# A tuned transformer-trunk kernel on one core: sums asked for later, V turned earlier, last rows normalised from halves

## The chip, the core and the metric

The kernel runs on one core of one Trainium2 chip. The metric is the device time of one launch in microseconds (us). The core's engines are TensorE (PE, with PEld for its weight loads), VectorE (DVE), ScalarE (ACT), GpSimd (POOL) and SyncE (SP, which here only starts transfers). ACT and POOL can start transfers too. A queue with a `q` behind the engine's name (SPq, POOLq) is the instruction stream that starts transfers.

## The reference

One layer over x of 2048 rows and 1024 columns, in fp32; `S` is 2048 and `D` 1024.

```python
mod = silu(c) @ w_ada + b_ada;  shift, scale, gate = split(mod, 3)
u = x * (1 + scale) + shift
q, k, v, a_gate, p_in, p_gate, m_a, m_p = split(u @ w_in)     # widths 1024 128 128 1024 1024 1024 1024 1024
a = sliding_window_sink_attention(q, k, v) * silu(a_gate)     # 16 heads of 64, 2 kv heads, window 128
p = (group_linear(multiscale_causal_pool(p_in), w_pool_mix) * pool_scale) * silu(p_gate)
y = sigmoid(m_a) * (a @ w_attn_proj) + sigmoid(m_p) * (p @ w_pool_proj)
y = (y @ w_out) * (1 + gate)
out = layer_norm(2**0.25 * x + y) * ln_gain + ln_bias
```

## The kernel before

**Products.** Every fp32 matrix is split into a high and a low part (fp32r), and a product of two 128x128x512 blocks is three matmuls (`mm3`: high by high, high by low, low by high). A large product is done in 2x2 blocks with seven products instead of eight. The class `Quad` (L262) holds the weights of one such 2x2 piece: two row tiles of 128 by 1024 columns, loaded by `load` (L270) as two pieces into a tile `W` (three blocks of 128x512) and one, the lower right one, into `A22` (the trace calls it `A`). `sum1` (L280, on POOL) adds two blocks, `mid` (L284, L285) subtracts twice and loads the fourth block by POOL's queue (L286), `late` (L290) subtracts once more. `pair_split` casts two blocks to the high part on ACT (L312) and takes the low part on DVE (L128) into `w_set`; `half_split` does so for `A22` (L319). `product` then runs twelve matmuls against one of seven resident moving sets (B11, T1, T2, B21, T3, B22, T4) in SBUF: `set_B` and `set_T` in the trace. There are two `W` and two `A22` buffers. `A22` lies in the phase's own pool for even groups (`own`); for odd ones it shares its two buffers with `mhi` and `mlo` of the fold described below.

**Groups and ticks.** Quads go in groups of two. `ring` (L421) runs over the groups: `back` does the products T2, B21, T3, B22, T4 of both quads, and `front` the products B11 and T1 of the next group's. A product is a tick, a group has 14. In `back`, the next quad's `load`, sum included, stands in the program beside the `pair_split` for T3 (`third`). `hooks` holds functions for a (group, tick); `defer` puts one some ticks ahead. `consume` of a quad takes each finished 512-column piece out of PSUM.

**Order.** Instructions given through `nc` are ordered by a list scheduler at build time by program order and readiness; those given through `sp`, `act`, `dve`, `pool` and `pe` keep the order of the program. Each engine then runs its list strictly in order. SP's transfers use eight completion counters in turn, so that one may wait for the eighth before it.

**Stages.** They follow in this order, with rough times of the trace: the head, until 55 us; `first_phase` for the first half of the sequence (K, V, attention gate, q, pool input and the other gates in nine groups; beside it the fold of the pool's mixing weights in groups 1, 3, 5 and 6, which ends in stores to `wmix_d` on POOL's queue), until 430; attention until 730; `second_phase` for the second half until 1045; attention until 1345; four mix phases (attention and pool projection by halves of the sequence, with the merge gates `ga` and `gp` and the results stored to `y_d`) until about 1690; the out phase with eight quads `out_quad`, two rows of 128 in each, which ends in the layer norm.

**Buffers of tag c.** Five tiles of 128x512 serve `sig`, `c12`, `vt`, `st_hi`, `st_lo`, `mr`, `k_hi` and `k_lo`. `vt` holds V transposed until `turn_v` (L605) turns it on the PE (four transposes into PSUM bank `pt` or `pv`), copies it on ACT (L610) and takes its low part on DVE into `vv`.

**Out phase.** The residual x rows are loaded by `load_z` into six wide tiles `zs`: rows 0 and 1 in the last mix phase, 2 to 5 ahead of the out ring, and row + 6 three ticks behind the store of a row. `out_quad.consume` adds the residual on DVE (L597). After both halves of a row, `norm_row` defers its steps: ACT sums the row, then the squares; the power -0.5 is taken on POOL, two wide operations on DVE scale the row, and a store of 512 KB follows at tick 5 (all L55, the line of the order-keeping helper).

Of the kernel before, what the change touches and what calls it, by code (L numbers as in the profile page):

```python
# [14 lines left out]
ALU = mybir.AluOpType  # L15
# [3 lines left out]
P = 128  # L19
# [3 lines left out]
CH = 512  # L23
# [9 lines left out]
EPS = 1e-5  # L33
# [25 lines left out]
def kernel(  # L59
# [22 lines left out]
    nc = tc.nc  # L82
# [37 lines left out]
    pin_d = [set_store(f"pin{s}") for s in range(2)]  # L120
    gates_d = {n: dp.tile([2, KT, 2, P, CH], F32, name=f"{n}_d") for n in ("ag", "pg", "ma", "mp")}
    y_d = dp.tile([S // P, P, KT, P], F32, name="y_d")

    def as32(ap):
        return ap.bitcast(F32)
# [223 lines left out]
    def back(ph, grp, opened, nxt, own, tick, b22_first=False):  # L349
        st = []  # L350
        for q, (a, b, c, w) in zip(grp, opened):
            u2, p5 = ph.p("u2"), ph.p("p5")
            nc.scalar.copy(u2, a)
            nc.scalar.copy(p5, b)
            if w is None:
                w = pair_split(ph, q.second())
                q.late()
            if c is None:
                c = bank("lg")
                product(c, w[1], "T2", True)  # L360
            tick()
            nc.vector.tensor_tensor(u2, c, u2, ALU.add)  # L362
            nc.gpsimd.tensor_tensor(p5, p5, u2, ALU.add)  # L363
            product(a, w[0], "B21")
            tick()
            q.consume(ph, 0, 0, a)
            st.append((q, b, c, u2, p5))
        w = {}

        def third(x):  # L370
            w[x] = pair_split(ph, st[x][0].third())
            if x < len(nxt):
                nxt[x].load(ph, own)

        def with_t3(x):
            q, b, c, u2, p5 = st[x]
            product(c, w[x][1], "T3", True)
            tick()
            nc.vector.tensor_tensor(p5, c, p5, ALU.add)
            q.consume(ph, 1, 1, p5)  # L380

        def with_b22(x):
            q, b, c, u2, p5 = st[x]
            product(b, w[x][0], "B22")
            tick()
            c12 = ph.c("c12")
            nc.vector.tensor_tensor(c12, b, u2, ALU.add)
            q.consume(ph, 0, 1, c12)

        if b22_first:  # L390
            for x in range(len(st)):
                third(x)
                with_b22(x)
            for x in range(len(st)):
                with_t3(x)
        else:
            for x in range(len(st)):
                third(x)
                with_t3(x)
                with_b22(x)  # L400
        for q in nxt[len(st) :]:
            q.load(ph, own)
        for q, b, c, u2, p5 in st:
            w = half_split(ph, q.a22)
            product(c, w, "T4")
            tick()
            nc.vector.tensor_tensor(u2, c, u2, ALU.add)  # L407
            q.consume(ph, 1, 0, u2)
# [3 lines left out]
    def defer(ticks, f):  # L412
        due.append((now[0] + ticks, len(due), f))
# [140 lines left out]
    zs = {}  # L554
# [6 lines left out]
    def norm_row(ph, row, z):  # L561


        def small(name):
            return ph.t.tile([P, 1], F32, tag=name, bufs=2, name=name)

        total, mean, down, rs = (small(x) for x in ("total", "mean", "down", "rs"))

        def sums():
            act.activation(z, z, AF.Copy, accum_out=total)  # L570

        def squares():
# [12 lines left out]
        def store():  # L585
            sp.dma_start(out[row * P : (row + 1) * P, :], z)
            defer(3, lambda: load_z(ph, row + 6))

        for at, f in ((1, sums), (2, squares), (3, power), (4, scale), (5, store)):
            defer(at, f)  # L590

    def out_quad(k):
        def consume(ph, mi, n, src):
            z, n_done = zs[k + mi]
            zs[k + mi][1] += 1
            zn = z[:, n * CH : (n + 1) * CH]
            nc.vector.scalar_tensor_tensor(zn, zn, ALPHA, src, ALU.mult, ALU.add)  # L597
            if n_done:
                norm_row(ph, k + mi, z)

        return Quad(tuple(y_d[k + i].rearrange("p k q -> p (k q)") for i in range(2)), consume)

# [445 lines left out]
    def cols(t, n):  # L1048
        return t[:, n * CH : (n + 1) * CH]

    def gate_modulation(ph, m, cb):
        wa = []

# [151 lines left out]
    def first_phase(ph, groups, turn, opened, cb, rest):  # L1205
        hooks = {}

        def at(group, pos, f):
            hooks.setdefault((group, pos), []).append(f)

        for g in range(4):
            steps(hooks, groups, (13, 41, 69, 92)[g], fold_parts(ph, g))
        for i in range(2):
            at(1, 1 + 2 * i, lambda i=i: turn(i))
        for j in range(KT):
            at(3 + j // 2, 3 + 5 * (j % 2), lambda j=j: spread_bias(j))
        for i in range(4):
            ks = (i, 4 + i)
            todo = sums_to(
                ph,  # L1220
                u1_d,
                i,
                lambda x, r, ks=ks: sp.dma_start(x, xt[1, ks[r]]),
                lambda x, r, ks=ks: modulate(x, ks[r]),
                True,
            )
            steps(hooks, groups, (1, 29, 57, 80)[i], todo)
        for i in range(8):
            steps(hooks, groups, 28 * (i // 2) + 20 + i % 2, gate_modulation(ph, 2 * KT + i, cb))
        for n, f in zip((0, 1, 3), rest):  # L1230
            at(0, n, f)
        for half in range(2):
            at(-1, 3 + half, lambda half=half: build(ph, "T2", half, b12_d))
        return ring(ph, groups, opened, hooks, [], lambda tick: first_q(ph, tick))

    def second_phase(ph, opened, groups, turn):
        hooks = {(1, 1 + 2 * i): [lambda i=i: turn(i)] for i in range(2)}
        for p, name, half in ((0, "T3", 0), (1, "T3", 1), (3, "T4", 0), (5, "T4", 1)):
            hooks.setdefault((0, p), []).append(lambda name=name, half=half: fill_set(name, half, u1_d[name]))
        cb = ph.t.tile([P, D], F32, tag="cb", bufs=1, name="cb")  # L1240
# [12 lines left out]
        for i in range(4):  # L1253
            ks = (i, 4 + i)
            todo = sums_to(
                ph,
                wo_d,
                i,
                lambda x, r, ks=ks: load_wo(x, ks[r]),
                lambda x, r: dve.tensor_tensor(x, x, cb, ALU.mult),  # L1260
                False,
            )
            steps(hooks, groups, 5 + 26.5 * i, todo)
            for n in range(4):
# [32 lines left out]
    ta, vec = {}, {}  # L1297
    with Pools("mix", spare=2, p=4, c=5) as ph:
# [9 lines left out]
        for i, (groups, store) in enumerate(phases):  # L1308
# [79 lines left out]
```

## Time and profile before

| | |
|---|---|
| time, median of 3 runs | 1850.66 us (1850.57 to 1857.23) |
| the profiled execution | 1849.77 us, its span 1848.0 us |
| mean granted clock of TensorE | 0.98 of full speed |
| PE busy | 1732.7 us (94%) |
| DVE, ACT, POOL busy | 1312.4, 942.6, 928.6 us |
| transfers | 381.32 MB, 206 GB/s over the span |

A row of a timeline reads: start, busy time, engine, source line, operation, out<-in, size, count, and in brackets the idle time of the engine just before it with what ended it. A row of the waits reads: who waited, for what, us in total, times, the longest. A row of the windows reads: the stretch, its length, busy time of PE, PEld, DVE, ACT and POOL with counts, the granted clock, the share of the DMA engines and GB/s. A row of the transfer issues reads: out<-in, queue, operation, count, KB each, and median us from issue to landing. Several equal operations in a row are joined in one row of a timeline.

### The profile page before, as it was taken

What the parts mean: (1) busy time and instruction counts of PE and PEld (TensorE: products, weight loads), DVE (VectorE), ACT (ScalarE), POOL (GpSimd) and SP (SyncE); (2) the same over time, 40 slices, a digit from 0 to 9 for tenths busy, and PEclk for the clock granted to TensorE, in tenths of its full rate; (3) what the DMA queues carried; (4) which work ended last, traced back from release to release, by engine and by line L of the source; (5) the groups of instructions that cost most, each with busy time, mean ns of one, the idle gap of its engine ahead of it and who ended that gap; (6) DMA issues with size and microseconds to landing.
All of it is one profiled execution on the core that took longest, in us unless ns stands there. A gap on an engine that the chain in (4) does not pass through costs nothing. (4 is left out here: it accounts for less than half of the span.)

```text
span 1848.0 us, 25300 instructions
## 1 busy us (share of the span) xinstructions
PE 1732.7 (94%) x8248; PEld 1437.6 (78%) x8248; DVE 1312.4 (71%) x2284; ACT 942.6 (51%) x1977; POOL 928.6 (50%) x758
## 2 busy tenths in 40 slices
PE   6789899999999999999999999999989989999996
PEld 6667677788888887787777888888867778777775
DVE  6955656554777777777766457777857887886886
ACT  4533334443777776543444367777724343422453
POOL 2234445451354667445445224456754785476553
PEclk9889999999999999999999999999999999999998
DMA  9245556677254457785776733543876574589432
GB/s 354 97 167 177 205 199 230 233 234 196 93 170 143 153 170 295 264 283 204 261 255 248 253 118 125 177 160 121 301 280 216 174 259 171 200 296 384 147 141 102
DMA packets 163571, 381.32 MB, mean 206 GB/s; under 512 B 19680, under 2 KB 23792, under 8 KB 163440
## 3 DMA queue, kind: packets, MB, share of 16 engines
q1 hardware_dynamic: 150528, 342.95, 53.3%
q0 software_dynamic: 10112, 33.06, 5.2%
q10 hardware_dynamic: 2800, 3.70, 0.9%
q8 instruction: 65, 1.06, 0.2%
q14 instruction: 66, 0.54, 0.1%
HBM read 244.35 MB, written 138.44 MB: 207 GB/s over the span
## 5 line engine op out<-in xcount | busy, mean ns | idle before, releaser
L55 PE MATMUL mm<-set_B,w_set 128*128 128x512 f32 x3240 | 809.6, 398 | 33.7 <-DVE w_set L128 23.3
L55 PEld LDWEIGHTS mm<-set_B,w_set 128*128 128x128 f32 x3240 | 606.8, 191 | 169.5 <-DVE w_set L128 32.4
L55 PE MATMUL lg<-set_T,w_set 128*128 128x512 f32 x2088 | 523.0, 400 | 49.5 <-ACT w_set L312 18.2
L55 PEld LDWEIGHTS lg<-set_T,w_set 128*128 128x128 f32 x2088 | 395.7, 192 | 152.6 <-DVE w_set L128 29.5
L128 DVE TENSOR_TENSOR w_set<-W,w_set 128x1024 fp32r<-128x1024 f32 x162 | 241.2, 1489 | 142.5 <-ACT w_set L312 137.4
L312 ACT CAST w_set<-W 128x1024 fp32r<-128x1024 f32 x162 | 169.5, 1050 | 234.6 <-PE mm L55 159.8
L55 PE MATMUL mm<-set_T,w_set 128*128 128x512 f32 x1080 | 267.1, 395 | 0.0
L55 PEld LDWEIGHTS mm<-set_T,w_set 128*128 128x128 f32 x1080 | 202.4, 190 | 42.2 <-DVE nxt L55 0.2
L284 POOL TENSOR_TENSOR W<-W 128x512 f32<-128x512 f32 x56 | 85.2, 1522 | 148.3 <-DVE w_set L128 129.0
L290 POOL TENSOR_TENSOR W<-W 128x512 f32<-128x512 f32 x56 | 80.1, 1430 | 157.8 <-DVE w_set L128 146.4
L363 POOL TENSOR_TENSOR p<-p,u 128x512 f32<-128x512 f32 x58 | 98.0, 1693 | 93.6 <-DVE u L362 91.4
L280 POOL TENSOR_TENSOR W<-W,A 128x512 f32<-128x512 f32 x56 | 82.5, 1473 | 109.1 <-DMA A<-in_win_dram 46.4
L55 DVE TENSOR_TENSOR o<-pv,o 64x128 f32<-64x128 f32 x256 | 72.4, 283 | 90.0 <-ACT o L55 87.1
L55 ACT ACTIVATE L<-L,nm 128x257 f32<-128x257 f32 (+1 forms) x256 | 127.8, 501 | 8.5 <-DVE nm L55 3.2
L55 DVE TENSOR_TENSOR k_lo<-spare,k_hi 128x512 fp32r<-128x512 f32 x88 | 89.7, 1027 | 48.4 <-ACT k_hi L55 24.4
L55 DVE CUSTOM_DVE_ANT_0 L<-lg,bt,nsink 128x256 f32<-128x256 f32 (+1 forms) x256 | 111.6, 473 | 5.3 <-PE lg L55 1.2
L285 POOL TENSOR_TENSOR W<-W 128x512 f32<-128x512 f32 x56 | 90.0, 1610 | 12.1 <-DMA W<-in_win_dram 9.5
L55 POOL TENSOR_TENSOR w_set<-W,w_set 128x1024 fp32r<-128x1024 f32 x14 | 33.7, 2408 | 122.8 <-ACT w_set L55 54.7
L55 POOL TENSOR_TENSOR p<-nxt,pg 128x512 f32<-128x512 f32 x32 | 41.4, 1294 | 105.1 <-DVE sm L55 103.8
L55 ACT COPY o<-pv 64x256 f32<-64x256 f32 x128 | 47.4, 371 | 80.8 <-PE pv L55 78.6
L55 DVE TENSOR_TENSOR ptl<-pt,pth 128x512 fp32r<-128x512 f32 (+1 forms) x128 | 85.8, 670 | 1.8 <-ACT pth L55 1.6
L55 ACT CAST k_hi<-spare 128x512 fp32r<-128x512 f32 x88 | 53.6, 616 | 55.2 <-POOL spare L55 20.3
(201 smaller groups left out, 2520.1 us busy)
## 6 DMA issues: line engine op xcount, KB each, us to landing
W<-in_win_dram SPq DMA_DIRECT2D x68, 256.0 KB, 3.8
w_set<-wmix_d SPq DMA_DIRECT2D x32, 512.0 KB, 5.4
A<-in_win_dram SPq DMA_DIRECT2D x34, 256.0 KB, 3.8
W<-in_win_dram POOLq DMA_DIRECT2D x34, 256.0 KB, 3.8
ag_d<-sig SPq DMA_DIRECT2D x32, 256.0 KB, 3.0
pg_d<-sig SPq DMA_DIRECT2D x32, 256.0 KB, 3.1
ma_d<-sig SPq DMA_DIRECT2D x32, 256.0 KB, 3.5
mp_d<-sig SPq DMA_DIRECT2D x32, 256.0 KB, 3.4
```

The costliest lines, as they stand in the source:

```text
L55: return lambda *args, **kw: self.tc.keep_in_program_order(op(*args, **kw))
L128: engine.tensor_tensor(dst, src, as32(hi), ALU.subtract)
L280: e.tensor_tensor(self.w[:, 1, :], self.w[:, 2, :], self.a22, ALU.add)
L284: e.tensor_tensor(x[:, 1, :], x[:, 1, :], x[:, 0, :], ALU.subtract)
L285: e.tensor_tensor(x[:, 2, :], x[:, 0, :], x[:, 2, :], ALU.subtract)
L290: e.tensor_tensor(x[:, 0, :], x[:, 0, :], x[:, 1, :], ALU.subtract)
L312: a.copy(by_two(hi), raw)
L363: nc.gpsimd.tensor_tensor(p5, p5, u2, ALU.add)
```

## The change

Four edits. First, `back` asks for the next quad's blocks by `ask`: the load is deferred by one tick and the sum by three, where both stood at the T3 split of the current quad; this holds in all rings. Second, V is turned in group 0 of both first phases, at ticks 7 and 10 (first) and 8 and 10 (second), where it was turned in group 1 at ticks 1 and 3. Third, rows 13 to 15 of the output take their statistics on DVE by halves (`bn_stats` as each half arrives, then `bn_aggr`), are scaled as a whole and then by halves, and each half is stored at once, one by SP and one by ACT's queue; the other rows keep the sums on ACT, with their store a tick later. Fourth, residual rows 2 to 5 are loaded at ticks 1, 1, 5 and 5 of the out phase's first group. `cols` only moves; it shifts the lines below it (L280 is L283 after), while L55 stays.

```diff
@@ back
+        def ask(q):
+            defer(1, lambda: q.load(ph, own, e=None))
+            defer(3, lambda: q.sum1(nc.gpsimd))
+
         def third(x):
             w[x] = pair_split(ph, st[x][0].third())
             if x < len(nxt):
-                nxt[x].load(ph, own)
+                ask(nxt[x])
...
         for q in nxt[len(st) :]:
-            q.load(ph, own)
+            ask(q)
@@ norm_row
-        for at, f in ((1, sums), (2, squares), (3, power), (4, scale), (5, store)):
+        for at, f in ((1, sums), (2, squares), (3, power), (4, scale), (6, store)):
             defer(at, f)
+
+    def last_stats(row, n, zn):
+        nc.vector.bn_stats(carry[:, row - 12, 6 * n : 6 * n + 6], zn)
+
+    def last_norm(row, z):
+        st, mv, rs = (carry[:, row - 12, a:b] for a, b in ((0, 12), (12, 14), (14, 15)))
+        nc.vector.bn_aggr(mv, st)
+        nc.vector.tensor_scalar(rs, mv[:, 1:2], EPS, None, ALU.add)
+        nc.gpsimd.tensor_tensor(rs, rs, mhalf, ALU.pow)
+        nc.vector.scalar_tensor_tensor(z, z, mv[:, 0:1], vec["gain"], ALU.subtract, ALU.mult)
+        for n, q in enumerate((nc.sync, nc.scalar)):
+            zn = cols(z, n)
+            nc.vector.scalar_tensor_tensor(zn, zn, rs, cols(vec["lnb"], n), ALU.mult, ALU.add)
+            q.dma_start(out[row * P : (row + 1) * P, n * CH : (n + 1) * CH], zn)
@@ out_quad.consume
             nc.vector.scalar_tensor_tensor(zn, zn, ALPHA, src, ALU.mult, ALU.add)
+            if row > 12:
+                last_stats(row, n, zn)
             if n_done:
-                norm_row(ph, k + mi, z)
+                if row > 12:
+                    last_norm(row, z)
+                else:
+                    norm_row(ph, row, z)
@@ first_phase
         for i in range(2):
-            at(1, 1 + 2 * i, lambda i=i: turn(i))
+            at(0, (7, 10)[i], lambda i=i: turn(i))
@@ second_phase
-        hooks = {(1, 1 + 2 * i): [lambda i=i: turn(i)] for i in range(2)}
+        hooks = {(0, (8, 10)[i]): [lambda i=i: turn(i)] for i in range(2)}
@@ mix and out phases
-                for row in range(2, 6):
-                    load_z(ph, row)
+                for at, row in ((1, 2), (1, 3), (5, 4), (5, 5)):
+                    hooks.setdefault((0, at), []).append(lambda row=row: load_z(ph, row))
```

More of the change, by code (lines that the diff above doesn't have):

```diff
@@ L122, with cols @@
     y_d = dp.tile([S // P, P, KT, P], F32, name="y_d")
+    def cols(t, n):
+        return t[:, n * CH : (n + 1) * CH]
     def as32(ap):
@@ L587, in store @@
             defer(3, lambda: load_z(ph, row + 6))
-        for at, f in ((1, sums), (2, squares), (3, power), (4, scale), (5, store)):
+        for at, f in ((1, sums), (2, squares), (3, power), (4, scale), (6, store)):
             defer(at, f)
+    def last_stats(row, n, zn):
[10 more added lines that the diff above has]
+            q.dma_start(out[row * P : (row + 1) * P, n * CH : (n + 1) * CH], zn)
     def out_quad(k):
         def consume(ph, mi, n, src):
-            z, n_done = zs[k + mi]
-            zs[k + mi][1] += 1
-            zn = z[:, n * CH : (n + 1) * CH]
+            row = k + mi
+            z, n_done = zs[row]
+            zs[row][1] += 1
+            zn = cols(z, n)
             nc.vector.scalar_tensor_tensor(zn, zn, ALPHA, src, ALU.mult, ALU.add)
+            if row > 12:
+                last_stats(row, n, zn)
             if n_done:
-                norm_row(ph, k + mi, z)
+                if row > 12:
+                    last_norm(row, z)
+                else:
+                    norm_row(ph, row, z)
         return Quad(tuple(y_d[k + i].rearrange("p k q -> p (k q)") for i in range(2)), consume)
@@ L1046, in gate_quads @@
         return groups, turn
-    def cols(t, n):
-        return t[:, n * CH : (n + 1) * CH]
     def gate_modulation(ph, m, cb):
```

## The prediction

> **What bounds the kernel now.** I read the page first, for the shares of the engines and the largest groups; then the waits of the PE, for what ends its idle time; then the PE's timeline, for where each wait lies; then the timelines of the engines that end these waits; last the order in which the two kernels issue their instructions on each engine, which says what the change really moves.
>
> ```profile
> span 1848.0 us, 25300 instructions
> PE 1732.7 (94%) x8248; PEld 1437.6 (78%) x8248; DVE 1312.4 (71%) x2284; ACT 942.6 (51%) x1977; POOL 928.6 (50%) x758
> PE mm L55 <- DVE w_set L128: 23.3, 19, 3.7
> PE lg L55 <- ACT w_set L312: 18.2, 11, 5.1
> 1417.78 2.88 PE L55 MATMUL mm<-set_T,w_set 128*128 128x512 f32 x12
> 1420.50 0.61 PE L55 MATMUL mm<-set_B,w_set 128*128 128x512 f32 x2
> ```
>
> The PE is busy for 94% of the span and the change leaves its matmuls as they are, so all there is to win is idle time of the PE: 115 us in all, part of it in the head, which isn't touched. It is spread over many short waits for weights (a `w_set` that ACT casts at L312 and DVE completes at L128) and two fills of the moving sets. The last two rows give the length of a product, which is a tick: the next one starts 1420.50 − 1417.78 = 2.72 us later. So the question is which of the waits the change reaches. The run in which these rows were taken was 1849.77 us, 1.77 over its span and 0.89 under the median of 1850.66; I sum against it and add 0.9 at the end. A measurement of this kernel can tell about 0.5% (9.25 us) from no change.
>
> **Part 1, sum1 three ticks later, first phase, groups 1, 3, 5.** In the order lists, deferring the sum moves POOL's L280 really only here: from ahead of four `wmix_d` stores of the fold to behind three of them.
>
> ```profile
> L280 POOL TENSOR_TENSOR W<-W,A 128x512 f32<-128x512 f32 x56 | 82.5, 1473 | 109.1 <-DMA A<-in_win_dram 46.4
> 138.82 1.29 POOL L280 TENSOR_TENSOR W<-W,A 128x512 f32<-128x512 f32 x1 [10.59 <-DMA A<-in_win_dram]
> 140.06 0.73 POOL L55 DMA_DIRECT2D wmix_d<-st_hi  x1
> 142.24 0.73 POOL L55 DMA_DIRECT2D wmix_d<-st_lo  x1
> 137.16 0.58 ACT L55 CAST st_hi<-pt 128x512 fp32r<-128x512 f32 x1
> 149.12 0.63 ACT L517 ACTIVATE sig<-c 128x512 f32<-128x512 f32 x1 [9.15 <-DMA wmix_d<-st_lo]
> 150.63 1.03 ACT L312 CAST w_set<-W 128x1024 fp32r<-128x1024 f32 x1
> 151.72 0.73 PE L55 MATMUL mm<-set_B,w_set 128*128 128x512 f32 x2 [1.70 <-ACT w_set L312]
> 153.24 2.08 PE L55 MATMUL mm<-set_B,w_set 128*128 128x512 f32 x4 [0.80 <-DVE w_set L128]
> 249.57 0.73 PE L55 MATMUL mm<-set_B,w_set 128*128 128x512 f32 x2 [1.83 <-ACT w_set L312]
> 251.16 1.37 PE L55 MATMUL mm<-set_B,w_set 128*128 128x512 f32 x3 [0.85 <-DVE w_set L128]
> 342.86 0.73 PE L55 MATMUL mm<-set_B,w_set 128*128 128x512 f32 x2 [2.78 <-ACT w_set L312]
> 344.11 1.22 PE L55 MATMUL mm<-set_B,w_set 128*128 128x512 f32 x2 [0.53 <-DVE w_set L128]
> ```
>
> Read upwards from the PE: it waits at 151.72 for ACT's cast, ACT came to it late because it had stood 9.15 us at a `sig` that needs one of the five `c` buffers, and that buffer came free only when a `wmix_d` store landed. The stores had been ready soon after the cast at 137.16 but stood on POOL's queue behind the sum at 138.82, which itself had waited 10.59 for its load. With the sum behind them they issue 2 to 5 us earlier, and ACT's cast is no longer late. The idle time in the three groups is 2.50 + 2.68 + 3.31 = 8.49 us. Not all need go: behind a cast that is only just late DVE's half costs the PE 0.53 of its own (344.11), and about as much for the cast itself, in three groups 3.2. So the gain is 5.3 to 8.5; I take **7.0**, near the full end because the buffer comes over 4 us sooner and the PE waited under 3. The load goes out a tick later, which is covered by its own wait for a buffer (the 10.59).
>
> **Part 2, V turned in group 0.** Two of the five `c` buffers no longer hold `vt` through group 1.
>
> ```profile
> 97.94 0.62 ACT L504 COPY vt<-u 128x512 f32<-128x512 f32 x1 [1.60 <-DMA u_B_split<-k_lo]
> 99.84 1.43 PE L55 MATMUL mm<-set_B,w_set 128*128 128x512 f32 x5 [1.86 <-DVE w_set L128]
> 114.61 0.62 ACT L55 CAST k_hi<-spare 128x512 fp32r<-128x512 f32 x1 [6.74 <-DMA u_T_split<-k_hi]
> 117.70 1.22 PE L55 MATMUL lg<-set_T,w_set 128*128 128x512 f32 x2 [5.08 <-ACT w_set L312]
> 215.27 0.73 PE L55 MATMUL lg<-set_T,w_set 128*128 128x512 f32 x2 [3.09 <-ACT w_set L312]
> 309.17 0.73 PE L55 MATMUL lg<-set_T,w_set 128*128 128x512 f32 x2 [1.38 <-ACT w_set L312]
> ```
>
> The 5.08 at 117.70 is ACT waiting 6.74 for a `c` buffer ahead of `k_hi`. Groups 3 and 5 have the same place without `vt`, and still lose 3.09 and 1.38 there, so I take the mean of what would be left, 2.2, and a gain of **2.5**, a little under 5.08 − 2.24 = 2.8 (2.0 to 3.7). Against it: the transposes leave a place near 130 where they filled about 0.5 of a wait (**−0.5**). In group 0 the PE already waits 1.86 for DVE at 99.84, DVE gets two more `vv` operations there (256 elements, so under the 0.69 that a row of 512 takes in part 5), and the PE reaches the second transpose a product ahead of that wait, at 99.84 − 1.86 − 2.72 = 95.3, while `vt` is copied only at 97.94 to 98.56: up to 3.3 us of a new wait, in whose shadow the 1.86 disappears. Net cost between 0 and 2.6; I take **−1.0**, since a freed buffer also shortens the 1.60. In the second phase the turn finds `vt` long ready: nothing.
>
> **Part 3, order of the fills.** Deferring the loads lets a fill that was queued behind them on SP go ahead.
>
> ```profile
> 743.72 0.38 SPq L194 DMA_DIRECT2D set_T<-u_T_split  x1
> 754.04 2.50 PE L55 MATMUL lg<-set_T,w_set 128*128 128x512 f32 x5 [2.90 <-DMA set_T<-u_T_split]
> 1675.21 14.88 SPq L55 DMA_DIRECT2D wide<-in_xr_dram  x4
> 1690.20 0.93 SPq L194 DMA_DIRECT2D set_B<-wo_B_split  x2
> 1697.77 2.12 PE L55 MATMUL mm<-set_B,w_set 128*128 128x512 f32 x6 [3.58 <-DMA set_B<-wo_B_split]
> 1700.34 2.02 PE L55 MATMUL mm<-set_B,w_set 128*128 128x512 f32 x4 [0.45 <-DMA set_B<-wo_B_split]
> ```
>
> In the second phase the last T4 fill now issues ahead of the three loads of the next group's second quad (768 KB, about 2 us at the rates below): up to 2.90 gained, but those loads now stand behind a `sig` store which waits for DVE, so their front may be up to 2 us late; I take **1.9** (0 to 2.9). In the out phase four residual rows occupied SP from 1675.21 for 14.88 us and the B22 fill stood behind them; now the fill stands ahead of all four: 3.58 + 0.45 = **4.0** (2 to 4.0). What is late next there: residual rows 2 and 3, which DVE needs with the group's first results, and the T4 fills behind them.
>
> **Part 4, mix phases.** At three boundaries between mix phases the order lists put the second front `w_set` on DVE ahead of a `set_B` split, a `set_T` split and two modulations, where it stood behind them.
>
> ```profile
> 1417.15 1.21 DVE L55 TENSOR_TENSOR set_B<-spare,set_B 128x1024 fp32r<-128x1024 f32 x1
> 1422.49 1.88 PE L55 MATMUL mm<-set_B,w_set 128*128 128x512 f32 x7 [1.37 <-DVE w_set L128]
> 1512.73 1.65 PE L55 MATMUL mm<-set_B,w_set 128*128 128x512 f32 x6 [1.57 <-DVE w_set L128]
> 1592.77 1.43 PE L55 MATMUL mm<-set_B,w_set 128*128 128x512 f32 x5 [1.39 <-DVE w_set L128]
> ```
>
> These three waits go, 4.33 us, since over 3 us of DVE work leaves the path; but one `u` of 0.6 moves ahead of the first front `w_set`, which was late already: −1.8. Net **2.5** (0 to 4.3).
>
> **Part 5, the last rows.**
>
> ```profile
> 1832.16 0.69 DVE L407 TENSOR_TENSOR u<-lg,u 128x512 f32<-128x512 f32 x1
> 1841.53 1.46 POOL L55 TENSOR_TENSOR rs<-rs,mhalf 128x1 f32<-128x1 f32 x1 [1.53 <-DVE rs L55]
> 1843.02 1.28 DVE L55 SCALAR_TENSOR_TENSOR wide<-wide,rs,wide 128x1024 f32<-128x1024 f32 x1 [0.44 <-POOL rs L55]
> 1670.00:1680.00 10.00, 10.00 (x46) 8.28 (x45) 7.17 (x6) 2.61 (x4) 8.63 (x9) 1.00 1.03 412
> ```
>
> The power on POOL and the wide operations on DVE alternate, about 3 us a row. Before, from 1832.16 DVE had 12.1 us of work and waits left, to 1844.30, and the span ended 3.7 later, with one store of 512 KB behind it. After, the list leaves from the same place two u and two L597 (0.6 each, an estimate from the row's 0.69 less the 0.09 by which neighbours overlap), four wide operations (1.2, from 1.28 in the same way), six half ones (0.6), two `bn_stats` and about 0.5 of small ones, and 0.4 of waiting for the last power: 1.2 + 1.2 + 4.8 + 3.6 + 1.2 + 0.9 = 12.9, so DVE ends 0.8 later. No row shows `bn_stats`: it reads 512 elements, so 0.6 by the row of `u` as the lower bound, and 1.28, a wide operation's, as the upper; I take the lower, the row of the same size, and the other end makes it 1.4 worse. That ACT's two wide passes a row vanish gains little, as POOL's power (1.46) and DVE set the pace of these rows. What is in flight at the end grows: row 12's whole store now stands on SP behind row 15's first half, so 256 + 512 + 256 KB are under way where 512 KB were, at 412 GB/s (the last number of the window's row) 1.3 us more, half of it beside DVE's last operation. Sum **−1.5** (from +1 to −3.5).
>
> The Trainium skill ("DMA: Bandwidth & Descriptors", section "Issuing engines are not separate DMA queues") says that transfers started by different engines run on the same sixteen DMA engines, and that a second issuing engine saves only issue time; no row here shows two queues storing halves at the same time. By this rule splitting a store over SP and ACT buys no rate; if each queue had a rate of its own, the last half would be clear of row 12's store and the tail would be −0.8 instead of −1.5.
>
> **Sum.** 7.0 + 2.5 − 0.5 − 1.0 + 1.9 + 4.0 + 2.5 − 1.5 = 14.9 us gained: 1849.8 − 14.9 = 1834.9 for the profiled run, and 0.9 more for the median, **1835.8**. With the poor ends of all terms it is 5.3 + 2.0 − 0.5 − 2.6 + 0 + 2 + 0 − 3.5 = 2.7, with the good ones 8.5 + 3.7 − 0.5 + 2.9 + 4.0 + 4.3 + 1 = 23.9; they won't all fall on one side, and the forecast's own range is 1829 to 1841.
>
> **Rivals.**
>
> *The next wait takes over in the first phase.* ACT's cast needs the sums on POOL too, and these now start three ticks later; if they end no sooner than the buffer came free before, the PE waits as long, for POOL. For it: 46.4 us of POOL's waiting for loads, in front of this very sum. Against: the sum at 138.82 lies twelve us ahead of the cast at 150.63, and the two sums behind it take 1.3 each. The gains of part 1 and of `k_hi` go: 14.9 − 9.5 = 5.4 gained, 1845.3; no difference that can be told. Chance 0.20.
>
> *The edits do less than the order says.* With the DMA engines full (the last row of part 5's fence: ten us of the out phase at 412 GB/s, its last column), a fill that issues earlier lands earlier only as far as bytes ahead of it shrink, and a `w_set` that is moved up may not have its cast yet. Then parts 3 and 4 give nothing: 14.9 − 8.4 = 6.5 gained, 1844.2. For it: the full engines. Against: the B22 fill was 14.9 us late at the queue, not on the wire. Chance 0.10.
>
> *Loads too late everywhere: slower.* Load and sum are now two ticks apart, 5.4 us.
>
> ```profile
> A<-in_win_dram SPq DMA_DIRECT2D x34, 256.0 KB, 3.8
> ```
>
> As long as a load lands in 5.4 us it is there when the sum's turn comes; the median of 3.8 says so. Where the engines are full it isn't (10.59 of waiting at 138.82), and a front that is a whole tick late costs 2.72. From nine such groups of the 28 (56 sums, two a group) on the kernel is slower: 9 × 2.72 = 24.5 more than forecast, 1860.3. Against it: POOL's order outside the three groups hardly changes, and there the sum waits for other things than its load. Chance 0.08.
>
> **How the numbers follow.** The forecast has 0.60; a gain beyond its range, 0.02. Faster by over 0.5% (under 1841.4): 0.62; within it, both middle rivals: 0.30; slower by over 0.5%: 0.08. The range that holds 8 in 10 runs from 1829, the good end, to 1846, which takes in both middle rivals.
>
> **What would show it.** In the profile after: the `wmix_d` stores of groups 1, 3 and 5 issue ahead of L283's sum, and the waits near 151, 249 and 343 shrink under 0.6 each; the wait near 118 falls to about 2; a new wait of the PE of 2 to 3 us stands near 96 in place of that at 99.84; the PE's wait for `set_T<-u_T_split` goes or falls under 1, its two waits for `set_B<-wo_B_split` go; the second waits of the mix boundaries go; the span ends 4 to 6 us after DVE's last operation instead of 3.7. Wrong it is if POOL's sums become the releaser near 151, 249 and 343, if waits for `set_T` or residual rows appear near 1700, or if fronts wait for loads in the mix phases.

## The result and the profile after

The changed kernel takes 1824.5 us in the median of four runs (1823.62 to 1827.09), the kernel before 1850.62 in the same comparison: the ratio is 0.9862 with a 95% interval of 0.9842 to 0.9882, so 26 us or 1.4% faster. The forecast was 1835.8 and its range ended at 1829.0: right in sign, and 11 us too small. On another chip the ratio came out as 0.9874 (0.9853 to 0.9895, run f1 below).

First the page of the changed kernel and the waits of its PE.

```profile
span 1822.9 us, 25301 instructions
PE 1722.4 (94%) x8248; PEld 1432.9 (79%) x8248; DVE 1315.4 (72%) x2290; ACT 933.8 (51%) x1965; POOL 929.5 (51%) x758
PE mm L55 <- DVE w_set L131: 22.0, 13, 2.9
PE lg L55 <- DVE w_set L131: 16.7, 19, 5.5
PE lg L55 <- ACT w_set L315: 13.5, 9, 3.7
PE lg L55 <- DMA set_T<-u_T_split: 1.6, 1, 1.6
```

The span is 25.1 us shorter. Idle time of the PE fell by 115.3 − 100.5 = 14.8. The other 10.3 is in the first number of the second row: the PE was busy for 1722.4 where it had been busy for 1732.7, with the same 8248 matmuls. The matmuls themselves took less time, and the prediction had no term for that. The windows view says where; here are 55 to 430 us, the first phase, of the kernel before, and then of the changed one (the columns are those of the row for 1670 us in the prediction; the clock is the third number from the end):

```profile
55.00:430.00 375.00, 341.46 (x1494) 275.63 (x1495) 232.53 (x272) 154.72 (x235) 168.69 (x139) 0.95 0.57 195
```

```profile
55.00:430.00 375.00, 354.39 (x1587) 287.54 (x1587) 249.00 (x286) 162.41 (x246) 174.57 (x140) 0.98 0.62 207
```

In the same 375 us there are 93 matmuls more, and the granted clock is 0.98 instead of 0.95. From 50 us on the traces hold only two values of this clock, 1.00 and 0.50. Over all stretches at 0.50 in the span the PE was busy for 55.3 us before and for 40.1 in the changed kernel (the windows view again); half of the difference, 7.6 us, is most of the 10.3.

The PE runs the same matmuls in both traces, apart from the place of V's transposes, so the start of the k-th matmul in one can be set against the k-th in the other, and the steps of this difference say where time was won. The table has them by place, in us won: the forecast, the changed kernel against the kernel before, a second execution of the changed kernel (run f1), and, as a measure of what differs in any case, a second execution of the kernel before (run g2), all against the first profile of the kernel before.

| place | forecast | changed | changed again | before again |
|---|---|---|---|---|
| head | 0 | 1.2 | 0.6 | 0.2 |
| groups 1, 3, 5 of the first phase, at the stores to `wmix_d` | 7.0 | 15.6 | 15.1 | 1.2 |
| group 0, and group 1 up to 145 us | 1.0 | 4.0 | 3.9 | 0.9 |
| rest of the first phase | 0 | 0.6 | −1.0 | 1.5 |
| second phase, with both attentions | 1.9 | 0.1 | −2.2 | −1.7 |
| mix phases | 2.5 | 3.0 | 5.9 | −1.9 |
| out phase, to the last matmul | 4.0 | 2.5 | 3.7 | −1.1 |
| behind the last matmul | −1.5 | −1.8 | −1.8 | 0.1 |
| sum | 14.9 | 25.1 | 24.1 | −0.8 |

The first phase won 12 us more than forecast and the head 1 more; the places behind them gave 3 less. In the second phase and the mix phases two executions of one kernel differ by 2 to 3 us, so single waits there prove nothing; in groups 1, 3 and 5 they agree within 1.3 each.

Now the first of the three places, group 1 of the changed kernel, engine by engine.

```profile
130.58 0.72 POOL L55 DMA_DIRECT2D wmix_d<-st_hi  x1 [7.47 <-ACT st_hi L55]
131.36 0.72 POOL L55 DMA_DIRECT2D wmix_d<-st_lo  x1
132.92 0.72 POOL L55 DMA_DIRECT2D wmix_d<-st_hi  x1 [0.83 <-ACT st_hi L55]
136.64 1.28 POOL L283 TENSOR_TENSOR W<-W,A 128x512 f32<-128x512 f32 x1 [3.00 <-DMA A<-in_win_dram]
137.88 0.72 POOL L55 DMA_DIRECT2D wmix_d<-st_lo  x1
135.42 0.63 ACT L525 ACTIVATE sig<-c 128x512 f32<-128x512 f32 x1 [0.57 <-DMA wmix_d<-st_hi]
140.20 1.03 ACT L315 CAST w_set<-W 128x1024 fp32r<-128x1024 f32 x1
139.21 5.67 PE L55 MATMUL lg<-set_T,w_set 128*128 128x512 f32 x24
144.72 2.93 PE L55 MATMUL mm<-set_B,w_set 128*128 128x512 f32 x12
```

The order is the forecast one: three stores, the sum, the last store. ACT's `sig` waits 0.57 for a buffer where it waited 9.15, its next cast comes at 140.20, over 4 us ahead of the product at 144.72 that needs it, and the PE's rows have no wait in brackets. The waits of groups 3 and 5 at the same place are gone too. In group 0 the new wait that I feared is this:

```profile
94.97 0.62 ACT L512 COPY vt<-u 128x512 f32<-128x512 f32 x1
95.64 0.66 PE L55 MATMUL pt<-ident,vt 128*128 128x128 f32 x4 [0.32 <-ACT vt L512]
112.93 1.09 PE L55 MATMUL lg<-set_T,w_set 128*128 128x512 f32 x2 [2.33 <-ACT w_set L315]
```

The first `vt` was turned three products earlier and has given its buffer back, so the copy of the second doesn't wait (it waited 1.60) and comes 3 us earlier, and the PE waits 0.32. The 1.86 at 99.84 doesn't come back. Where 5.08 stood at 117.70 there is 2.33 now.

### The profile page after: what moved, and what is told of

Same layout as the page of the kernel before. It is cut to its first block, busy times and chain, and to the rows that moved or that the text cites. A ratio compares the mean times of both kernels' runs of the same rounds, so it can differ in the third digit from the quotient of the medians.

```text
span 1822.9 us, 25301 instructions
## 1 busy us (share of the span) xinstructions
PE 1722.4 (94%) x8248; PEld 1432.9 (79%) x8248; DVE 1315.4 (72%) x2290; ACT 933.8 (51%) x1965; POOL 929.5 (51%) x758
## 5 line engine op out<-in xcount | busy, mean ns | idle before, releaser
L55 PE MATMUL mm<-set_B,w_set 128*128 128x512 f32 x3240 | 802.1, 396 | 22.2 <-DVE w_set L131 22.0
L55 PEld LDWEIGHTS mm<-set_B,w_set 128*128 128x128 f32 x3240 | 602.9, 189 | 154.0 <-DVE w_set L131 30.3
L55 PE MATMUL lg<-set_T,w_set 128*128 128x512 f32 x2088 | 521.9, 400 | 44.3 <-DVE w_set L131 16.7
L55 PEld LDWEIGHTS lg<-set_T,w_set 128*128 128x128 f32 x2088 | 396.0, 192 | 146.2 <-DVE w_set L131 27.0
L55 PE MATMUL mm<-set_T,w_set 128*128 128x512 f32 x1080 | 266.4, 395 | 0.0
L55 PEld LDWEIGHTS mm<-set_T,w_set 128*128 128x128 f32 x1080 | 201.3, 189 | 41.6
L55 DVE TENSOR_TENSOR o<-pv,o 64x128 f32<-64x128 f32 x256 | 72.4, 283 | 93.2 <-ACT o L55 90.5
L55 ACT ACTIVATE L<-L,nm 128x257 f32<-128x257 f32 (+1 forms) x256 | 127.1, 498 | 8.4 <-DVE nm L55 3.3
L283 POOL TENSOR_TENSOR W<-W,A 128x512 f32<-128x512 f32 x56 | 82.7, 1476 | 86.9 <-DMA W<-in_win_dram 20.2
L55 DVE TENSOR_TENSOR k_lo<-spare,k_hi 128x512 fp32r<-128x512 f32 x88 | 92.4, 1058 | 47.8 <-ACT k_hi L55 24.0
L55 DVE CUSTOM_DVE_ANT_0 L<-lg,bt,nsink 128x256 f32<-128x256 f32 (+1 forms) x256 | 111.6, 473 | 5.3 <-PE lg L55 1.3
L288 POOL TENSOR_TENSOR W<-W 128x512 f32<-128x512 f32 x56 | 90.4, 1614 | 15.1 <-DMA W<-in_win_dram 12.3
L55 POOL TENSOR_TENSOR w_set<-W,w_set 128x1024 fp32r<-128x1024 f32 x14 | 33.7, 2405 | 122.8 <-ACT w_set L55 89.7
L55 POOL TENSOR_TENSOR p<-nxt,pg 128x512 f32<-128x512 f32 x32 | 41.3, 1291 | 104.6 <-DVE sm L55 104.6
L55 ACT COPY o<-pv 64x256 f32<-64x256 f32 x128 | 47.3, 370 | 82.3 <-PE pv L55 80.2
L55 DVE TENSOR_TENSOR ptl<-pt,pth 128x512 fp32r<-128x512 f32 (+1 forms) x128 | 85.7, 669 | 1.7 <-ACT pth L55 1.6
L55 ACT CAST k_hi<-spare 128x512 fp32r<-128x512 f32 x88 | 53.4, 615 | 60.4 <-POOL spare L55 32.3
```

The lines of the kernel that those rows point to most:

```text
L55: return lambda *args, **kw: self.tc.keep_in_program_order(op(*args, **kw))
L283: e.tensor_tensor(self.w[:, 1, :], self.w[:, 2, :], self.a22, ALU.add)
L288: e.tensor_tensor(x[:, 2, :], x[:, 0, :], x[:, 2, :], ALU.subtract)
```

## The experiments

All are made from one of the two kernels. Steps in us are steps of the PE against the first profile of the kernel before, as in the table.

**What a wait of the PE costs.** My theory after the result: a wait costs its idle time, and from some length on also a stretch in which the PE runs at half rate. The changed kernel got added waits in smooth stretches of the second phase:

```diff
+        lag = ph.t.tile([P, P], F32, tag="lag", bufs=1, name="lag")
+        def stall(n):
+            a, b = bank("pt"), bank("pv")
+            pe.transpose(a[:, 0:P], lag, ident)
+            act.copy(lag, a[:, 0:P])
+            for _ in range(n):
+                act.copy(lag, lag)
+            pe.transpose(b[:, 0:P], lag, ident)
+        for at, n in (((3, 6), 3), ((5, 5), 9), ((6, 6), 20)):
+            hooks.setdefault(at, []).append(lambda n=n: stall(n))
```

> The changed kernel with three added waits of the PE in smooth stretches of the second phase (a chain of 3, 9 and 20 small ACT copies between two added transposes in groups 3, 5 and 6; the results are not used). Theory A (after a wait of over about 2.3 us the PE runs at half rate for some us): the waits will be about 1.2, 2.7 and 5.5 us of idle, and the matmuls behind them cost 0.1, 1.5 and 1.5 to 3 us more than at full rate, 1824.5 + 9.5 + 4 = 1838. Rival B (a wait costs its idle time): 1834, and the spacing of matmuls behind all three is 0.227.

The ratio to the kernel before was 0.9957 (0.9939 to 0.9975), in the profile 15 us over the changed kernel, near the 15.3 of idle time, since a later wait near 877 all but went. The copies took longer than I had reckoned. The timeline of the PE at the three waits:

```profile
855.68 0.33 PE L55 MATMUL pv<-ident,lag 128*128 128x128 f32 x1 [1.95 <-ACT lag L55]
855.77 2.54 PE L55 MATMUL mm<-set_B,w_set 128*128 128x512 f32 x10
936.80 0.48 PE L55 MATMUL pv<-ident,lag 128*128 128x128 f32 x1 [4.72 <-ACT lag L55]
936.93 4.23 PE L55 MATMUL lg<-set_T,w_set 128*128 128x512 f32 x12
941.00 2.89 PE L55 MATMUL mm<-set_B,w_set 128*128 128x512 f32 x12
988.00 0.48 PE L55 MATMUL pv<-ident,lag 128*128 128x128 f32 x1 [8.64 <-ACT lag L55]
988.13 4.23 PE L55 MATMUL mm<-set_B,w_set 128*128 128x512 f32 x12
```

Behind 1.95 us of waiting the matmuls run at their usual pace (2.54 for ten). Behind 4.72 twelve take 4.23 where they take 2.89 a product later, and behind 8.64 also 4.23. So the rival falls: a long wait costs about 1.35 us over its idle time, and a longer one no more than that. Where the step lies was still open, and it decides for waits of 2 to 3.5 us like those that the change removed. The same kernel with seven waits of 4 to 7 copies:

```diff
-        for at, n in (((3, 6), 3), ((5, 5), 9), ((6, 6), 20)):
+        for at, n in (((3, 6), 4), ((3, 11), 5), ((4, 6), 6), ((4, 11), 5), ((5, 5), 4), ((5, 10), 6), ((6, 6), 7)):
```

> The changed kernel with seven added waits of the PE in the second phase (chains of 4 to 7 small ACT copies, so about 2.4, 2.9, 3.3 and 3.8 us of idle, by the 1.95 of three copies and the 4.72 of nine in the run of stalls; the results are not used). Theory A (half rate follows from some length on): a wait of 2.4 is followed by matmuls at 0.23 us each, one of 3.8 by a stretch at 0.45 that costs 1.3 us more, and the step lies between. Rival (the extra cost grows with the wait): 0.3 to 1 us behind the middle ones.

```profile
884.42 0.48 PE L55 MATMUL pv<-ident,lag 128*128 128x128 f32 x1 [3.55 <-ACT lag L55]
884.55 5.47 PE L55 MATMUL mm<-set_B,w_set 128*128 128x512 f32 x12
965.25 0.33 PE L55 MATMUL pv<-ident,lag 128*128 128x128 f32 x1 [3.07 <-ACT lag L55]
965.34 4.59 PE L55 MATMUL lg<-set_T,w_set 128*128 128x512 f32 x12
983.64 0.33 PE L55 MATMUL pv<-ident,lag 128*128 128x128 f32 x1 [2.71 <-ACT lag L55]
983.72 3.00 PE L55 MATMUL mm<-set_T,w_set 128*128 128x512 f32 x12
```

2.71 costs nothing more, 3.07 costs 1.7 and 3.55 costs 2.9 (half rate for a whole product and on into the next). The four others, of 4.35 to 5.32, cost 1.5 to 2.9, with no order by length. So length alone doesn't decide. The granted clock does: in each trace, from 50 us on, it changes only on a grid of 3.41 us, which runs on whatever the PE does. Here are stretches of that grid (the first number behind the comma is the PE's busy time), around the 3.07 and the 2.71 of this run, and then in the kernel before around its wait of 1.86 at 99.84:

```profile
962.17:965.58 3.41, 0.34 (x3) 0.33 (x3) 3.41 (x4) 3.00 (x9) 2.86 (x2) 1.00 0.72 263
965.58:969.00 3.42, 3.42 (x9) 2.64 (x9) 1.01 (x2) 0.00 (x0) 0.00 (x0) 0.50 0.91 285
979.23:982.65 3.42, 1.70 (x8) 1.10 (x7) 1.42 (x2) 2.44 (x8) 2.30 (x2) 1.00 1.02 397
982.65:986.06 3.41, 2.42 (x11) 2.04 (x12) 1.29 (x2) 2.44 (x6) 0.05 (x1) 1.00 0.78 276
```

```profile
97.91:101.32 3.41, 1.55 (x7) 1.24 (x7) 2.93 (x5) 2.46 (x5) 1.39 (x1) 1.00 0.47 169
101.32:104.73 3.41, 3.41 (x9) 2.65 (x8) 0.77 (x2) 1.96 (x3) 2.07 (x3) 0.50 0.61 208
```

The wait of 3.07 left the PE 0.34 us of work in one stretch, and the next is at half clock. The wait of 2.71 fell across a border, left 1.70 and 2.42, and nothing followed. The shorter wait of 1.86 fell into one stretch, left 1.55, and half clock followed. In the 16 traces on record, counted from 55 us to about 16 us before the end, all 111 stretches at full clock in which the PE was idle for over 60% of the time are followed by one at half clock, 57 of the 196 with 40 to 60%, and none of the 7711 with less. So what decides is the share of a stretch that goes idle, and where a wait falls on the grid differs between executions. The price is half of the PE's work in the one or two stretches at half clock: 1.7 us for a full one, and 1.35 behind 4.72 and 8.64, because these waits reached into the stretch themselves.

**Which edit does what in the first phase.** V's turn alone (`ask` replaced by the old `load`, and the out phase as before), and `ask` alone (the turn and the out phase as before):

> The kernel before with V turned in group 0 and nothing else. Theory A (the two edits act at different places): about 1 us in group 0 and 3 to 4 near 117, so 1846, and the waits near 151, 249 and 343 stay as before (about 2.5, 2.7, 3.3 us of idle). Rival B (buffers of tag c are short in group 1 as a whole, and the turn is what frees them): the wait near 151 goes too, 6 us more, so 1840.

> The kernel before with load and sum deferred in all rings and nothing else. Theory A: 5.9 + 4.8 + 5.2 = 16 us in groups 1, 3 and 5, 5 in the mix phases, nothing net in the second phase, so 1830; the wait near 117 stays. Rival B (group 1 needs the turned V): 6 us less, 1836, with a wait near 151 left.

The turn alone: ratio 0.9995 (0.998 to 1.001), no difference. `ask` alone: 0.9896 (0.988 to 0.9911). The PE's timeline with the turn alone, at groups 1, 3 and 5:

```profile
146.64 0.73 PE L55 MATMUL mm<-set_B,w_set 128*128 128x512 f32 x2 [1.50 <-ACT w_set L315]
242.91 0.73 PE L55 MATMUL mm<-set_B,w_set 128*128 128x512 f32 x2 [2.83 <-ACT w_set L315]
334.50 0.73 PE L55 MATMUL mm<-set_B,w_set 128*128 128x512 f32 x2 [1.70 <-ACT w_set L315]
```

and with `ask` alone, at the wait near 118 and at group 1:

```profile
116.38 1.22 PE L55 MATMUL lg<-set_T,w_set 128*128 128x512 f32 x2 [4.46 <-ACT w_set L315]
147.18 3.00 PE L55 MATMUL lg<-set_T,w_set 128*128 128x512 f32 x12 [1.03 <-DVE p L387]
```

The turn wins 1.6 in group 0 and 3.3 near 118, and leaves the three later waits (the first is 1.50 us where 1.70 stood). `ask` wins 3.6, 4.8 and 5.2 at these three and leaves the wait near 118. So the two act at different places, as theory A had it, and add up: in group 1 the turn's own 1.5 comes on top of `ask`'s 3.6, where the two together win 5.6. That the turn's 4 us do not show in its time is a miss of my expectation: its profile wins 8.4 us up to the end of the first phase, but loses 7.9 behind it against the first profile of the kernel before; the second execution of that kernel loses 4.7 there too. The other 3 us, most of them in the out phase, stay open.

The sum alone deferred, the load at its old place, on the kernel before; and the load at its old place in the changed kernel:

```diff
-            defer(1, lambda: q.load(ph, own, e=None))
+            q.load(ph, own, e=None)
             defer(3, lambda: q.sum1(nc.gpsimd))
```

> The kernel before with the sum deferred by three ticks, the load left where it was. Theory A (what counts in the first phase is that the sum stands behind the stores): 16 us in groups 1, 3 and 5; the wait for the T4 fill near 754 stays; so 1834 or, if the mix phases gain too, 1830. Rival (the deferred load counts): under 5 us, 1846.

> The changed kernel with the loads not deferred, the sum still three ticks later. Theory A (deferred loads gain the T4 fill in the second phase and lose as much later in it): the wait near 731 is 1 us longer with half rate behind it, the waits near 789 and 877 are shorter: no difference, 1824.5. Rival B (late loads only cost): 3 us faster, 1821.5.

They gave 0.9939 (0.9922 to 0.9955) and 0.991 (0.9883 to 0.9936). The sum's place alone wins 5.3, 3.2 and 3.2 in groups 1, 3 and 5. That is less than the 16 I expected, but most of the 15.6, so the rival (that the deferred load counts there) falls; the deferred load adds 1.6 to 2 in each of groups 3 and 5. But in the other phases I was wrong on the load: without its tick the wait for the T4 fill is back at 3.43 us, and the mix phases win 0.8 instead of 3.0 to 5.9. On the load's tick in the second phase itself theory A stands: over the profiles of these runs, the place of the T4 fill wins 2.4 us on the mean with the tick (nine profiles, without that of the seven waits) and −0.4 without (five), and the rest of that phase loses 5.4 with it (eight, without the two runs with added waits) and 2.4 without (five). What was won there is lost again.

`ask` only in the first phase (`FIRST` is its name), the changed kernel otherwise:

```diff
+            if ph.name == FIRST:
                 defer(1, lambda: q.load(ph, own, e=None))
                 defer(3, lambda: q.sum1(nc.gpsimd))
+            else:
+                q.load(ph, own)
```

> The changed kernel with load and sum deferred only in the first phase. Theory A: the mix phases lose 5 us, the second phase and the out phase are even: 1829.5. Rival B (outside the first phase the deferral does as much harm as good): 1824.5.

0.9904 (0.9873 to 0.9934), 8 us behind the changed kernel's 0.9862 with intervals that overlap a little; in the profile the mix phases lose 2.7 against the kernel before, where the changed kernel wins 3.0. Over all profiles the mix phases win 2.6 to 6.7 in the ten with load and sum deferred there, lose 1.9 to 2.7 in the three with neither, and are between −0.1 and 0.8 in the two with the sum alone. Theory A stands: `ask` wins 5 us or so in the mix phases too.

**The out phase.** The residual rows loaded ahead of the ring as before, and the deferral taken from the out phase's own groups (`quad.soon = k >= 4` makes `ask` load and sum at once):

> The changed kernel with residual rows 2 to 5 loaded ahead of the out ring as before. Theory A (what the earlier fill gains is lost again to the wait near 1687, which comes of the rows' later loads): the wait for the B22 fill is back, 5 us, and the wait of 3.2 near 1687 falls to 1.5: 0 to 2 us slower, 1825.5. Rival B (the wait near 1687 comes of the deferred sums): 5 us slower, 1829.5.

> The changed kernel, but the out phase's own groups load and sum as before (not deferred). Theory A (deferred loads wait for full DMA engines, so the front of the out phase's second group is late): the wait of 3.2 near 1687 goes, the wait for the B22 fill stays away, 3 to 4 us faster than the changed kernel. Rival B (the wait near 1687 is DVE's norm work and is there in any case): no difference.

The rows as before gave 0.9877 (0.9852 to 0.9903), no difference that can be told from 0.9862. In the profiles, the wait near 1687 of the changed kernel, of the kernel with old rows, and of the one without deferral in these groups, in this order:

```profile
1686.67 3.66 PE L55 MATMUL mm<-set_B,w_set 128*128 128x512 f32 x8 [2.85 <-DVE w_set L131]
```

```profile
1677.02 1.66 PE L55 MATMUL mm<-set_B,w_set 128*128 128x512 f32 x6 [1.41 <-DMA set_B<-wo_B_split]
1679.58 1.66 PE L55 MATMUL mm<-set_B,w_set 128*128 128x512 f32 x6 [0.90 <-DMA set_B<-wo_B_split]
1695.47 2.57 PE L55 MATMUL mm<-set_B,w_set 128*128 128x512 f32 x10 [2.90 <-DVE w_set L131]
```

```profile
1691.59 2.58 PE L55 MATMUL mm<-set_B,w_set 128*128 128x512 f32 x10 [1.62 <-DVE w_set L131]
```

The rows' later loads win the B22 fill (5.9 us against the kernel before where old rows with `ask` win 3.0), and they don't make the wait near 1687: with old rows it is there as well. My theory A for e6 falls, the rival B stands: it comes of the deferral. Without it the wait is 1.62. The single waits are a weak sign, since the second execution of the changed kernel (f1) has 1.88 here. The steps are clearer: between 1705 and 1715 us of the kernel before, the nine profiles with the out phase's sums deferred lose 2.1 to 4.2 us, the six without lose nothing. Two of the nine have the load at its old place and lose 2.8 and 3.6, so it is the sum's deferral and not the load's. POOL's sum in the changed kernel:

```profile
1676.29 1.29 POOL L283 TENSOR_TENSOR W<-W,A 128x512 f32<-128x512 f32 x1 [9.27 <-DMA A<-y_d]
```

It waits 9.27 us for its load, but 9.24 with the load at its old place (e7) and 7.36 without any deferral (f2), so this wait doesn't tell them apart, and by which path the late sum reaches the PE is not shown. The time without the deferral was 0.9868 (0.9847 to 0.989) where the changed kernel had 0.9874 on that chip: 1 to 2 us in the profile, where 3 to 4 were expected, and nothing that the measurement can tell.

**The end.** The last rows as before in the changed kernel, also together with the last edit, and that edit with the halves kept and the store's old tick:

> The changed kernel with the last rows and the store tick as before. Theory A: the end behind the last matmul is 14.5 us again instead of 16.3, and the waits of 2.2 and 2.0 near 1728 and 1769 fall to 1.4: 2 to 3 us faster than the changed kernel, 1822. Rival B (the halves do shorten the end, and other things lengthened it): 1 to 2 us slower, 1826.

> As the one before, and the last rows and the store tick as in the kernel before. Theory A: 3 to 4 us in the out phase and 2 to 3 at the end, 6 us faster than the changed kernel (ratio to the kernel before 0.983). Rival: the tail is even, 3 us.

> As the run f2 with only the store tick back at 5, the last rows by halves. Theory A (the later store is what lengthened the waits near 1728 and 1769 from 1.4 to 2.1, by the residual row that follows it; the halves lengthen the end by 1.8): 1 us faster than f2, 2 us slower than f3. Rival (statistics on DVE are in the way there): as f2.

The ratios are 0.9856 (0.9824 to 0.9889), 0.9882 (0.986 to 0.9905) and 0.9875 (0.9853 to 0.9896): no difference from the changed kernel in any. In the profiles the time from the start of the last matmul to the end of the span is 14.4 to 14.5 us in all seven profiles with the old tail and 16.3 in all nine with the halves, so the halves cost 1.8 us every time. That is what I expected. In the times 1.8 us is 0.1%, less than these intervals can show, and other places differ by more (the head and the first phase of f3's profile, which no edit of it touches, are 5.5 us behind f1's). For the store's tick nothing was found: the wait near 1769 is 1.88 in f1 and still 1.46 in f3, and the out phase won 3.7 to 4.5 in f1 to f4. No version beat the changed kernel clear of noise.

**What differs between executions.**

> The changed kernel once more, for a direct comparison on this chip and to see what differs between executions of one kernel: the ratio near 0.986, the steps of the PE's clock against the kernel before within 1 us of the first profile in the first phase; in the second phase the wait near 877 may differ by some us if it hangs on when transfers land.

> The kernel before once more: by how much each place differs between two executions of one kernel. Theory A: under 1 us in the first phase, where the waits hang on order; up to 3 us in the second phase and the mix phases, where they hang on when transfers land. Rival (the waits of the first phase differ as much between executions as between the two kernels): 5 us or more in one of the groups 1, 3, 5.

The table above has both. Groups 3 and 5 repeat within 0.5 us, as theory A had it, and the rival falls. Group 1 differs by 1.3, a little over the forecast 1: its wait is followed by two stretches at half clock in the first profile of the kernel before and by one in the second (the clock from 155.57 on is 0.99).

## Why the prediction was right or wrong, step by step

**Part 1 is the step that failed.** The mechanism was right in each link: the stores ahead of the sum, the buffers free earlier (in the first phase ACT's `sig` waited 29.6 us for these stores, six times, and now 1.2, twice), ACT's cast no longer late. The price was wrong. "The idle time in the three groups is 2.50 + 2.68 + 3.31 = 8.49", and with it "the gain is 5.3 to 8.5", took the idle time as the most that could be won. It won 15.6 and 15.1. Two things are in the difference. First, the haircut for a cast "only just late" was for nothing: nothing is late there now. Second, the matmuls behind each of the three waits ran at half clock, and that ended too; the prediction put this at nothing. Here are the stretches at half clock behind the three waits in the kernel before:

```profile
152.52:155.93 3.41, 2.69 (x6) 2.15 (x7) 3.41 (x4) 1.77 (x3) 2.24 (x2) 0.50 0.35 131
155.93:159.35 3.42, 3.42 (x9) 2.64 (x8) 3.03 (x6) 1.22 (x2) 0.84 (x1) 0.50 0.42 153
251.51:254.92 3.41, 3.41 (x10) 2.65 (x9) 3.41 (x6) 0.70 (x2) 1.98 (x2) 0.50 0.30 109
343.67:347.08 3.41, 2.97 (x7) 2.39 (x8) 3.41 (x6) 1.77 (x3) 2.65 (x2) 0.50 0.83 287
```

The PE was busy for 12.49 us in them, and half of that, 6.2, is what the half clock cost. With the 8.49 of idle time this makes 14.7 of the 15.6; the last 0.9 is not accounted for. The changed kernel has no stretch at half clock at these places. Over the whole first phase the PE was busy at half clock for 31.7 us before and for 16.1 in the changed kernel, a cost of 15.8 and 8.0. The rows for it stood in the prediction: four matmuls in 2.08 at 153.24, three in 1.37 at 251.16, two in 1.22 at 344.11, against twelve in 2.88. The runs with added waits show that a wait makes this. In each of the three groups two waits of together 2.5 to 3.3, with two matmuls between them, fell mostly into one stretch of the grid. The half clock is there in the second execution of the kernel before as well, so it was no chance of one trace.

The Trainium skill ("TensorE: Matmul & The Clock Gate", section "What's actually happening") says that the array runs at half clock after an idle window of about 3.4 us and at full clock after a busy one, and that these windows run freely and don't start anew with a kernel. The trace agrees on the windows: stretches of 3.41 us on one grid, and a price that doesn't grow with the wait. It differs on how idle a window has to be: one with 1.55 us of work in its 3.41 was followed by half clock here.

**Part 2.** Forecast 1.0, measured 4.0. The gain near 118 was 3 instead of 2.5, and near 130 nothing was lost. The step that failed is "up to 3.3 us of a new wait": I put `vt`'s copy where it stood before, and counted the buffer that the same edit frees only as a reason not to take the worst end. The new wait was 0.32, and the old 1.86 went, with its half clock.

**Part 3.** The B22 fill gave 5.9, not 4.0, for the same reason as part 1 (half clock stands behind its wait, from 1698.76 to 1702.17); the out phase then lost 1 to 2 to the sums that POOL now does later, for which the forecast had no term. The T4 fill gave about 2.8, forecast up to 2.9, though 1.6 us of waiting for it is left where under 1 was forecast, and the rest of that phase gave back 3.5, where a third of it was forecast. So the term of 1.9 failed: the whole phase won 0.1, and −2.2 in the second execution.

**Part 4.** Forecast 2.5, measured 3.0 and 5.9. The second waits at the three boundaries went, as this stretch of the changed kernel shows (the wait of 1.37 stood behind the second matmul of the product that starts at 1400.12 now), and the first ones together are about as long as before (6.97 us where 6.54 stood), so that the 1.8 taken off was mostly not there. A new wait of 1.62 at 1474.74 took part of the gain, so the forecast's closeness to 3.0 is partly luck. The first of the three boundaries:

```profile
1394.96 2.60 PE L55 MATMUL mm<-set_B,w_set 128*128 128x512 f32 x10 [1.72 <-DVE w_set L131]
1400.12 2.88 PE L55 MATMUL mm<-set_B,w_set 128*128 128x512 f32 x12
```

**Part 5** held: −1.8 for −1.5. `bn_stats` was the lower bound (0.69), and DVE and the stores lengthen the end as reckoned:

```profile
1814.46 0.69 DVE L601 BATCH_NORM_STATS2 carry<-wide 128x6 f32<-128x512 f32 x1
1817.22 1.41 DVE L612 SCALAR_TENSOR_TENSOR wide<-wide,carry,wide 128x512 f32<-128x512 f32 x2 [0.44 <-POOL carry L608]
1818.38 0.42 SPq L55 DMA_DIRECT2D out_dram<-wide  x1
```

DVE ends at 1818.63, which is 1.2 us later behind the last matmul than before (0.8 was forecast), and 4.3 us later the span ends, where it was 3.7. Row 12's store leaves SP after row 15's first half.

**The rivals.** The next wait did not take over in the first phase (the sums are not late there). The edits do what the order lists said. That loads came too late is shown nowhere; the third rival falls. What no rival had is that a wait removed can be worth nearly twice its idle time, and the upper end of the range, in the direction of a gain, was drawn too near for it.

## What to carry to other kernels

Price a wait of the PE by the start of the first matmul behind it that runs at its usual pace again, not by the idle time: look at the busy time per matmul in the rows behind the wait, and at the granted clock of the stretch. A wait of a few us that goes may bring twice what the row in brackets says. Whether it does hangs on the clock's grid: 1.86 us inside one stretch of 3.41 was followed by half clock here, 2.71 across a border was not. So ask for windows of that length behind a wait before you price it. When many small waits differ between executions, set the two traces against each other matmul by matmul, and take a second execution of the same kernel before a place is given a cause.

## What the runs showed that I had not expected

The price of a wait doesn't go by its length: 1.35 us behind 4.72 and behind 8.64 us of idle time, 1.7 behind 3.07, 2.9 behind 3.55 and nothing behind 2.71, while half clock follows a wait of 1.86. The clock of a stretch of 3.41 us goes by how idle the PE was in the stretch before. And the second phase and the mix phases of one and the same kernel differ by up to 2.9 us between two executions, while groups 3 and 5 of the first phase repeat within 0.5 us. That the waits there hang on the order of a queue, and in the others on when transfers land, is my reading; no run shows it.
